# A state-space block's x projection: token-major products, turned by DMA transposes on ScalarE's queue

## The chip, the cores and the metric

The kernel runs on one core of one Trainium2 chip. The metric is device time in microseconds for one execution; the time of a kernel is the median of several runs. Engines are named as the profile names them: PE is TensorE (PEld its weight loads), DVE is VectorE, ACT is ScalarE, POOL is GpSimd, SP is SyncE, whose queue issues the weight loads. ACT has a DMA queue of its own (ACTq in the trace).

## The reference, cut to what matters

Two layers over 256 tokens of width 2048. Layer 0 is a differential attention, layer 1 a state-space mixer (Mamba-2); each is followed by a SwiGLU network. The change lies in the state-space mixer:

```python
proj = h @ w_in                                  # 256 x 2048 times 2048 x 10304
z, xbc, dt = jnp.split(proj, [4096, 10240], axis=-1)
xbc = silu(causal_conv(xbc, conv_w, width=4) + conv_b)   # per feature, along the tokens
xs, bm, cm = jnp.split(xbc, [4096, 5120], axis=-1)
...
y = ssd_chunked_scan(xs, dt, a, bm, cm)          # chunks of 128 tokens, 8 groups of 8 heads of 64
y = y + d_skip * xs
y = rms_norm(y * silu(z), norm_g)                # per group of 512 features
return y @ w_out
```

So of each of the 8 groups of 512 features, x is projected, convolved along the tokens, passed through silu, and used by tokens in the scan.

## The kernel before, in words

**Weight units.** All large products are split into three passes of reduced precision: a weight block is loaded by SP into one of seven buffers `raw` (128 x 1024, 512 KB), ACT copies it to a high part `wh` (`split_unit`, L260), and DVE subtracts to get the low part `wl`. `wh` and `wl` have four buffers each (`W_BUFS`), so ACT's copy for unit j+4 waits until PE has finished unit j. The activations have such a pair, `h` and `l` (`ah`, `al` in the trace). One unit covers 256 rows of the weight and 512 columns; a group's projection of 512 columns over 2048 rows is eight units.

**Two forms of a unit.** `products` (used by `push_k4`) keeps the activations stationary and streams the weights: 12 matmuls of 512 columns, and the result lies with tokens on the partitions. `feature_products` (used by `push_features`) keeps the weights stationary: 24 matmuls of 256 columns, and the result lies with features on the partitions. `Norm.push(..., features)` chooses: the fifth argument True gives the second form. In the first form the second matmul of a unit already reads `wl`; in the second the first 16 of 24 read `wh` alone.

**Order.** Everything is issued by one Python program, and each engine carries out its instructions in the order in which they were issued. Units enter a queue (`fifo`); `push_unit` issues the load and ACT's copy of a unit, and pops older units so that at most four wait. After the products of each popped unit `tick` runs one step of each generator in `active` (`step_all`), and, at a fixed rate, one of the `jobs` for the modulation vectors (one more `raw` load, and later a 128 x 1024 multiply on DVE, `raw<-raw,crow`). The subtraction for `wl` is issued one unit late (`lagging`, `low_parts`): that of unit j+3 is issued behind the step that follows unit j. Below, a step is the work issued after one unit, and step k of a group is the one after its k-th z unit; step 0 follows the last x unit.

**A group of the state-space stage.** Group g has eight x units (256-column form), `take_x` starts the generator `x_steps(g)`; then eight z units (512-column form), and `take_z` starts `y_steps(g)`. `x_steps` before: in steps 0 to 3 one tile of 128 features each goes through `conv_tile` (one ACT instruction from PSUM, L1555, three DVE instructions), in step 4 silu (L1565, with a load of ACT's function table ahead of it), in step 5 four PE transposes into a bank `wk`, and, once `y_steps(g-1)` is past its copies (`("done", g-1)`), two DVE multiplies; then the same for the second block of 128 tokens. `y_steps(g)` runs from step 8 on and into the next group: silu of z, 16 relu instructions in four steps, two exponentials with two DVE multiplies (`abc`), products `intra` on PE (the first in the next group's step 0), sums, two sums of squares (`square_sum`, steps 3 and 5), and from step 6 on the turning of y: ACT copies each y block's 32-bit words into two planes of 16-bit halves (L1772, `yT<-xsd`), and two `dma_start_transpose` on ACT's queue turn them into `yT` of the group (L1782). The place for the halves of group g is the not yet used `yT` of group g+1 (`y_turned(g+1)`).

**The output projection.** After z of group 7 come units (g, ch) of `ssd_out`, two units each, for groups g and output quarters ch. `split(cp, g)` prepares the stationary operand of a group ahead of it: for cp = 0 `y_words` first (two ACT copies that put the halves together, L383, and two DVE multiplies), then two ACT copies and two subtractions (L363). `split(0, 0)` is issued after the fourth z unit of group 7, `split(0, 1)` right after `take_z` of group 7, the next ones every four units. `flush_steps` runs all open generators to their end.

Of the kernel before, what the change touches and what calls it, by code (L numbers as in the profile page):

```python
# [11 lines left out]
F32 = mybir.dt.float32  # L12
# [3 lines left out]
U16 = mybir.dt.uint16  # L16
AF = mybir.ActivationFunctionType
# [75 lines left out]
def block_kernel(ctx: ExitStack, tc: tile.TileContext, x, x_t, columns_in, ssd_columns, da_columns, c, ada_w,  # L93
# [14 lines left out]
    pe, act, dve, pool, sp = nc.tensor, nc.scalar, nc.vector, nc.gpsimd, nc.sync  # L108
# [26 lines left out]
    rawp = ctx.enter_context(tc.tile_pool(name="rawp", bufs=RAW_BUFS))  # L135
# [8 lines left out]
    def bank(tag):  # L144
        return psum.tile([128, 512], F32, tag=tag, name=tag, bufs={"mm": 4, "wk": 3, "po": 1}[tag])

    def tmp(name="tmp"):
        return t2.tile([128, 512], F32, tag="t2", name=name)
# [19 lines left out]
    def take(what, n=1):  # L168
        while free[what] < n:
            yield  # L170
        free[what] -= n

    def give(what, n=1):
        free[what] += n
# [50 lines left out]
    def flush_steps():  # L225
        while active or pending:
            step_all()
# [131 lines left out]
    def split_act(parts):  # L359

        h, l = act_tiles()
        for at, src in parts:
            act.copy(at(h), src)  # L363
            dve.tensor_tensor(at(l), src, at(h).bitcast(F32), op=ALU.subtract)
        return blocks((h, l))
# [569 lines left out]
    wi = da_in  # L935
# [333 lines left out]
    for n in range(n_early, 12):  # L1269
        if n == n_early + 1:  # L1270
            call(load_x)
        hg, i = keys[n]
        bk = Banks()
# [251 lines left out]
    norm = Norm(0, mods["S", "m1"], mods["T", "m1"])  # L1525
# [23 lines left out]
    def tap(j, ct):  # L1549
        t = H[f"cw{j // 2}"]  # L1550
        i = (j % 2) * 48 + ct
        return t[:, i:i + 1]

    def conv_tile(src, d, ct):
        act.activation(d, src, AF.Identity, bias=H["cb"][:, ct:ct + 1], scale=tap(3, ct))  # L1555
        for j in range(3):
            m = 3 - j
            dve.scalar_tensor_tensor(d[:, m:], src[:, :256 - m], tap(j, ct), d[:, m:], op0=ALU.mult, op1=ALU.add)

    def conv_features(banks, n, dst, cts):  # L1560

        for k in range(n):
            conv_tile(banks[k // 2][:, (k % 2) * 256:(k % 2) * 256 + 256], dst[:, k, :], cts + k)
            yield
        act.activation(dst, dst, AF.Silu)  # L1565
        yield
# [99 lines left out]
    def hb(ap):  # L1666
        return ap[:, :, None].to_broadcast([128, 8, 64])

    def h3(ap):
        return ap.rearrange("p (h d) -> p h d", d=64)  # L1670

    def x_steps(g, banks):
        gp, h0 = S["gp"], 8 * g
        xc = gp.tile([128, 4, 256], F32, tag="xc", name="xc")
        yield from conv_features(banks, 4, xc, 4 * g)
        for b in range(2):
            yield from take("wk")
            ps = bank("wk")
            for i in range(4):
                pe.transpose(ps[:, i * 128:(i + 1) * 128], xc[:, i, b * 128:(b + 1) * 128], ident)  # L1680
            yield
            if b == 0:
                while g and ("done", g - 1) not in S:
                    yield
                xdt = S["xdt", g] = gp.tile([128, 2, 512], F32, tag="xdt", name="xdt")
                xsd = S["xsd", g] = gp.tile([128, 2, 512], F32, tag="xsd", name="xsd")
            dve.tensor_tensor(h3(xdt[:, b, :]), h3(ps), hb(S["dt"][:, b, h0:h0 + 8]), op=ALU.mult)
            dve.tensor_tensor(h3(xsd[:, b, :]), h3(ps), hb(H["dsk"][:, h0:h0 + 8]), op=ALU.mult)
            give("wk")
# [95 lines left out]
    def y_turned(g):  # L1785
        if ("yT", g) not in S:
            S["yT", g] = S["y0" if g < 4 else "y1"].tile([128, 2, 4, 128], F32, name=f"yT{g}")
        return S["yT", g]

    def half_tiles(t):  # L1790
        return t.rearrange("p k t -> p (k t)").bitcast(U16).rearrange("p (j t) -> p j t", t=128)
# [9 lines left out]
    wi = ssd_in  # L1801
    for col, n in ((9856, 448), (8192, 512), (8704, 384), (9088, 384), (9472, 384)):
        bk = Banks()
# [22 lines left out]
    hl = {}  # L1826

    def split(cp, g):
        if g == 7 and cp == 0:
            flush_steps()  # L1830
        if cp == 0:
            y_words(g)
        hl[cp, g] = split_act([(lambda t, b=b: t[:, :, b * 128:(b + 1) * 128], S["yT", g][:, b]) for b in range(2)])

    call(lambda: ada.update(rate=len(jobs) / ADA_UNITS))
    for g in range(8):
        bk = Banks()
        norm.push(wi, 4096 + g * 512, 512, bk, True)

        def take_x(g=g, bk=bk):  # L1840
            if g:
                step_until(xg[g - 1])
            xg[g] = start(x_steps(g, bk()))
        call(take_x)
        bk = Banks()
        norm.push(wi, g * 512, 512, bk, after=(lambda: split(0, 0)) if g == 7 else None)

        def take_z(g=g, bk=bk):
            yg[g] = start(y_steps(g, bk()))
        call(take_z)  # L1850
# [4 lines left out]
    def free_work():  # L1855
# [2 lines left out]
        phx = ExitStack()  # L1858
        nxt["xp"] = phx.enter_context(tc.tile_pool(name="xp_s", bufs=1))
        nxt["leave"] = lambda: (phx.close(), ph.close())  # L1860
    order = [(g, ch) for g in range(8) for ch in (0, 1)] + [(g, ch) for g in range(6) for ch in (2, 3)]
    order += [(6, 2), (7, 2), (6, 3), (7, 3)]
    bks = [Banks(t) for t in (("mm", "mm"), ("mm", "mm"), ("wk", "wk"), ("wk", "po"))]
    seen = []
    for g, ch in order:
        cp = ch // 2
# [5 lines left out]
    for g, ch in order:  # L1872
        cp = ch // 2
# [76 lines left out]
```

## Time and profile before

| | |
|---|---|
| median of 3 runs | 2609.04 us (2608.25 to 2609.65) |
| profiled execution: its time, its span | 2610.32 us, 2608.6 us |
| PE busy | 2584.8 us (99% of the span) |
| PEld / DVE / ACT / POOL busy | 2151.3 / 1914.4 / 1431.7 / 144.2 us |
| granted PE clock | 0.999 |
| DMA | 700.80 MB, mean 269 GB/s |
| state-space stage, groups 1 to 6 | 50.3 us each, PE busy throughout |

The profiled execution's time is its span and 1.7 us around it, and lies 1.3 us above the median. A busy sum adds up what overlaps inside an engine only once; the duration of one matmul in the trace (about 390 ns for 512 columns) is longer than the distance between two of them, since matmuls overlap. The rate of PE is therefore read from the chain of waits, where a row gives the start, the length and the number of matmuls in it.

### The profile page before, as it was taken

What the parts mean: (1) busy time and instruction counts of PE and PEld (TensorE: products, weight loads), DVE (VectorE), ACT (ScalarE), POOL (GpSimd) and SP (SyncE); (2) the same over time, 40 slices, a digit from 0 to 9 for tenths busy, and PEclk for the clock granted to TensorE, in tenths of its full rate; (3) what the DMA queues carried; (4) which work ended last, traced back from release to release, by engine and by line L of the source; (5) the groups of instructions that cost most, each with busy time, mean ns of one, the idle gap of its engine ahead of it and who ended that gap; (6) DMA issues with size and microseconds to landing.
All of it is one profiled execution on the core that took longest, in us unless ns stands there. A gap on an engine that the chain in (4) does not pass through costs nothing.

```text
span 2608.6 us, 35343 instructions
## 1 busy us (share of the span) xinstructions
PE 2584.8 (99%) x12914; PEld 2151.3 (82%) x12914; DVE 1914.4 (73%) x2621; ACT 1431.7 (55%) x1944; POOL 144.2 (6%) x227
## 2 busy tenths in 40 slices
PE   8999999999999999999999999999999999999999
PEld 5677778888888888888998899888888888888887
DVE  6778988778888867667777777786687664446775
ACT  4346654555654554446555676685545565545443
POOL 0014421000000000000000000010000000000000
PEclk9999999999999999999999999999999999999999
DMA  9977888698999988883667797876597687667885
GB/s 384 406 293 265 285 290 318 257 318 321 344 367 345 366 269 300 291 290 119 197 228 231 239 250 224 234 220 222 188 347 289 206 219 213 202 210 251 288 292 169
DMA packets 258206, 700.80 MB, mean 269 GB/s; under 512 B 86624, under 2 KB 95072, under 8 KB 256752
## 3 DMA queue, kind: packets, MB, share of 16 engines
q1 hardware_dynamic: 236176, 679.82, 76.4%
q10 hardware_dynamic: 17760, 4.43, 1.7%
q0 software_dynamic: 4096, 14.29, 1.6%
q8 instruction: 101, 1.65, 0.2%
q14 instruction: 73, 0.60, 0.1%
HBM read 680.53 MB, written 2.20 MB: 262 GB/s over the span
## 4 chain that ended last, share of the span: by engine, by line
PE 95%; DVE 2%; ACT 1%; issue 1%; DMA 1%; POOL 0%; POOLq 0%; ACTq 0%; DVEq 0%
PE mm L122 77%; PE wk L122 14%; PE po L122 5%; DVE wl L122 1%; DMA raw<-in_da_w_in 0%; DVE raw L122 0%; ACT wh L260 0%; ACT hm L563 0%; DVE xsum L122 0%; DVE partoh L122 0%; DVE x L122 0%; DVE hm L122 0%; DVE res L122 0%; POOL qr L415 0%; DVE qss L122 0%
## 5 line engine op out<-in xcount | busy, mean ns | idle before, releaser
L260 ACT CAST wh<-raw 128x1024 fp32r<-128x1024 f32 (+2 forms) x894 | 924.7, 1040 | 979.9 <-PE mm L122 615.3
L122 DVE TENSOR_TENSOR wl<-raw,wh 128x1024 fp32r<-128x1024 f32 (+2 forms) x894 | 1071.4, 1207 | 465.0 <-ACT wh L260 463.1
L122 PE MATMUL mm<-wh,ah 128*128 128x512 f32 (+1 forms) x2560 | 1012.0, 395 | 4.5 <-DVE partoh L122 2.9
L122 PE MATMUL mm<-wl,ah 128*128 128x512 f32 (+1 forms) x2560 | 997.9, 390 | 1.2 <-DVE wl L122 1.2
L122 PE MATMUL mm<-wh,al 128*128 128x512 f32 (+1 forms) x2560 | 998.9, 390 | 0.1
L122 PEld LDWEIGHTS mm<-wh,ah 128*128 128x128 f32 x2560 | 481.6, 188 | 130.3 <-issue 22.9
L122 PEld LDWEIGHTS mm<-wh,al 128*128 128x128 f32 x2560 | 481.4, 188 | 102.3 <-DVE al L122 1.3
L122 PEld LDWEIGHTS mm<-wl,ah 128*128 128x128 f32 x2560 | 481.9, 188 | 100.5 <-DVE wl L122 3.2
L122 DVE SCALAR_TENSOR_TENSOR raw<-raw,crow 128x1024 f32<-128x1024 f32 x320 | 389.7, 1220 | 0.0
L122 PE MATMUL wk<-wl,ah 128*128 128x512 f32 x360 | 140.1, 389 | 0.0
L122 PE MATMUL wk<-wh,al 128*128 128x512 f32 x360 | 140.1, 389 | 0.0
L122 PE MATMUL wk<-wh,ah 128*128 128x512 f32 x360 | 140.1, 389 | 0.0
L122 PE MATMUL mm<-ah,wh 128*128 128x256 f32 x720 | 118.8, 285 | 0.0
L122 PE MATMUL mm<-ah,wl 128*128 128x256 f32 x720 | 117.7, 283 | 0.0
L122 PE MATMUL mm<-al,wh 128*128 128x256 f32 x720 | 117.6, 283 | 0.0
L122 PEld LDWEIGHTS mm<-ah,wh 128*128 128x128 f32 x720 | 100.2, 192 | 0.1
L122 PEld LDWEIGHTS mm<-ah,wl 128*128 128x128 f32 x720 | 100.2, 192 | 0.0
L122 PEld LDWEIGHTS mm<-al,wh 128*128 128x128 f32 x720 | 100.1, 192 | 0.0
L505 POOL DMA_DIRECT2D gate_row<-grows x32 | 16.1, 509 | 1376.6 <-DVE grows L122 1376.6
L122 PEld LDWEIGHTS wk<-wl,ah 128*128 128x128 f32 x360 | 67.6, 188 | 14.2 <-DVE wl L122 0.2
L122 PEld LDWEIGHTS wk<-wh,al 128*128 128x128 f32 x360 | 67.6, 188 | 14.0
L122 PEld LDWEIGHTS wk<-wh,ah 128*128 128x128 f32 x360 | 67.6, 188 | 14.0
(331 smaller groups left out, 1998.3 us busy)
## 6 DMA issues: line engine op xcount, KB each, us to landing
raw<-in_ffn_w_gate_up SPq DMA_DIRECT2D x352, 512.0 KB, 4.9
raw<-in_ada_w SPq DMA_DIRECT2D x320, 512.0 KB, 5.2
raw<-in_ffn_w_down SPq DMA_DIRECT2D x176, 512.0 KB, 4.8
raw<-in_ssd_w_in SPq DMA_DIRECT2D x136, 512.0 KB, 4.5
raw<-in_da_w_in SPq DMA_DIRECT2D x90, 512.0 KB, 5.5
araw<-in_ada_w SPq DMA_DIRECT2D x64, 512.0 KB, 8.5
raw<-in_ssd_w_out SPq DMA_DIRECT2D x64, 512.0 KB, 4.4
raw<-in_da_w_out SPq DMA_DIRECT2D x32, 512.0 KB, 5.2
```

Source lines behind the costliest of these rows:

```text
L122: return fn(dst, *a, **k)
L260: act.copy(wh[:, at, :n], raw[:, at, :n])
L505: pool.dma_start(gate_dram[hf][:, 32 * q:32 * q + 32], rows[o:o + 8, :])
```

## The change

x of the state-space mixer is projected with tokens on the partitions (512-column form). `x_steps` then copies the two PSUM banks into halves (in the place of `xc`, which the convolution fills later), turns each block with a DMA transpose on ACT's queue, the second issued two steps after the first, puts the halves together with four ACT copies into two buffers `xin` of the common ring `t2`, and runs the convolution on these in two steps of two tiles, then silu, three empty steps, and the transposes on PE as before. The place for the turned halves is `y_turned(g+1)`, and for group 7 a buffer of `raw`. In the output projection group 7's first two quarters come after (0, 2) and (0, 3), and `flush_steps` is called at `split(1, 0)`.

```diff
     def x_steps(g, banks):
         xc = gp.tile([128, 4, 256], F32, tag="xc", name="xc")
-        yield from conv_features(banks, 4, xc, 4 * g)
+        hs = [xc[:, 2 * b:2 * b + 2, :].rearrange("p k t -> p (k t)").bitcast(U16) for b in range(2)]
+        for b in range(2):
+            act.copy(hs[b].rearrange("p (e f) -> p e f", e=2), banks[b].bitcast(U16).rearrange("p (f e) -> p e f", e=2))
+        if g < 7:
+            xT = [half_tiles(y_turned(g + 1)[:, b]) for b in range(2)]
+        else:
+            spare = rawp.tile([128, 2, 512], F32, tag="raw", name="xT")
+            xT = [half_tiles(spare[:, b].rearrange("p (k t) -> p k t", k=4)) for b in range(2)]
+        for b in range(2):
+            act.dma_start_transpose(xT[b], hs[b])
+            for _ in range(2 + b):
+                yield
+        for p in range(2):
+            xin = tmp("xin").rearrange("p (k t) -> p k t", k=2)
+            for b in range(2):
+                act.copy(xin[:, :, b * 128:(b + 1) * 128].bitcast(U16).rearrange("p k (t e) -> p k t e", e=2),
+                         xT[b].rearrange("p (e k) t -> p k t e", e=2)[:, 2 * p:2 * p + 2])
+            for i in range(2):
+                conv_tile(xin[:, i, :], xc[:, 2 * p + i, :], 4 * g + 2 * p + i)
+            yield
+        act.activation(xc, xc, AF.Silu)
+        yield
+        yield
+        yield
         for b in range(2):
             yield from take("wk")
...
-        if g == 7 and cp == 0:
+        if g == 0 and cp == 1:
             flush_steps()
...
-        norm.push(wi, 4096 + g * 512, 512, bk, True)
+        norm.push(wi, 4096 + g * 512, 512, bk)
...
-    order = [(g, ch) for g in range(8) for ch in (0, 1)] + [(g, ch) for g in range(6) for ch in (2, 3)]
+    order = [(g, ch) for g in range(7) for ch in (0, 1)] + [(0, 2), (0, 3), (7, 0), (7, 1)]
+    order += [(g, ch) for g in range(1, 6) for ch in (2, 3)]
     order += [(6, 2), (7, 2), (6, 3), (7, 3)]
```

## The prediction

> **What bounds the kernel now.** I read the page's first block, then the chain of waits, then the stage by windows, then the groups, tiles and timeline of ScalarE, because the first three say that only TensorE's own time counts here.
>
> ```profile
> span 2608.6 us, 35343 instructions
> PE 2584.8 (99%) x12914; PEld 2151.3 (82%) x12914; DVE 1914.4 (73%) x2621; ACT 1431.7 (55%) x1944; POOL 144.2 (6%) x227
> ```
>
> The profiled execution took 2610.32 us, its span 2608.6; the median of the runs is 2609.04. I make the sum against the profiled execution and subtract its 1.3 us at the end. PE is busy 99%. Two stretches of the chain give the price of both forms of a unit, and the windows show that the stage stands on PE alone:
>
> ```profile
> 978.42 10.88 PE mm L122 x48
> ...
> 1449.36 23.04 PE mm L122 x192
> ```
> ```profile
> core 0: us, PE busy (x) PEld busy (x) DVE busy (x) ACT busy (x) POOL busy (x), PEclk, DMA share, GB/s
> ...
> 1432.06:1482.36 50.30, 50.30 (x332) 45.80 (x331) 38.82 (x51) 32.98 (x50) 3.36 (x5) 1.00 0.78 243
> 1482.36:1532.65 50.29, 50.29 (x331) 45.79 (x331) 37.81 (x54) 32.96 (x50) 5.01 (x10) 1.00 0.87 228
> ```
>
> 48 matmuls of 512 columns take 10.88 us: 227 ns each, 2.72 us a unit of 12. The 192 matmuls of an x group take 23.04 us: 120 ns each, 2.88 us a unit of 24. A group is 50.3 us with no PE idle time; ACT is busy 33 of them, DVE 38, DMA for 0.78 to 0.87.
>
> **The change part by part.** *Products.* 64 x units go from 2.88 to 2.72 us: 64 x 0.16 = **10.2 us less** on PE, all on the path. The weights, their loads and copies are the same in number. PE's transposes, 8 a group, stay. That is the whole gain; the rest asks what makes PE wait.
>
> *ScalarE's bill.* These rows are of one group, and of all y tiles:
>
> ```profile
> L260 ACT CAST wh<-raw 128x1024 fp32r<-128x1024 f32 x17 | 17.8, 1047 | 18.6 <-PE mm L122 7.6 <-issue 7.6 <-DMA raw<-in_ssd_w_in 2.6
> L1555 ACT ACTIVATE xc<-mm,cb,cw 128x256 f32<-128x256 f32 x4 | 2.2, 557 | 1.6 <-DVE xc L122 1.6
> L1772 ACT COPY yT<-xsd 128x1024 uint16<-128x1024 uint16 x2 | 2.1, 1040 | 0.0
> L1565 ACT ACT_TABLE_LOAD x1 | 1.3, 1283 | 0.0
> L422 ACT ACTIVATE junk<-xsd 128x512 f32<-128x512 f32 x2 | 1.3, 626 | 0.0
> L1565 ACT ACTIVATE xc<-xc 128x1024 f32<-128x1024 f32 x1 | 1.1, 1061 | 0.0
> L1708 ACT ACTIVATE abc<-abc,acum 128x128 f32<-128x128 f32 x16 | 5.1, 393 | 0.2 <-issue 0.2
> ```
> ```profile
> L363 ACT CAST ah<-yT x32: 603/616/633, 1692.8 to 1860.8; 128x512 fp32r<-128x512 f32 x32
> L383 ACT COPY yw<-yT x16: 1157/1167/1185, 1690.6 to 1774.3; 128x1024 uint16<-128x1024 uint16 x16
> ...
> DMA to landing us min/median/max: 3.2/7.3/14.4
> ```
> ```profile
> L122 DVE SCALAR_TENSOR_TENSOR raw<-raw,crow 128x1024 f32<-128x1024 f32 x4 | 4.9, 1218 | 0.0
> L122 DVE SCALAR_TENSOR_TENSOR xc<-mm,cw,xc 128x255 f32<-128x255 f32 x4 | 1.9, 483 | 0.1
> ```
>
> Successive ACT records overlap by some 0.1 us (three copies in a row further down: 2.92 us, 0.96 each), so I count 0.96 for a copy of 1.05 and 1.2 for four relus. Added per group: two copies into halves, 0.95 each, and four copies that put halves together, each half of an L383 row: 0.55, 2.2 in all. The first pair falls in steps 0 to 4, where ACT waits for PE anyway: free. But in steps 5 to 7 there now stand the 2.2 us, the four convolution instructions (0.5 each, 2.0 in all, until now in steps 0 to 3), and table load with silu (2.25, until now in step 4). So 6.5 us more lie in three steps of 2.72 us, which already hold a weight copy each, a sum of squares (0.7) and a copy of y's halves (0.95). ACT can't work ahead: the copy of unit j+4 waits for PE's unit j, and what follows waits behind it.
>
> *A steady group.* Count from the end of z unit 4, when ACT copies unit 8. ACT: copy 0.96, squares 0.7, two xin copies 1.1, two convolution instructions 1.0, copy of unit 9 0.96, y's halves 0.95, 1.1, 1.0: 7.8 us. Behind the last but one of these DVE does two convolutions of three instructions (1.43 each by distance): 7.3 + 2.9 = 10.2, then `wl` of unit 9 (1.13, issued behind step 6): 11.3. PE wants that `wl` with its second matmul of unit 9, the next group's first x unit: 4 x 2.72 + 0.23 = 11.1. So 0.3 us late, or 1.5 where one of the four modulation multiplies of a group (1.22) falls in these steps. Before, the x unit's first 16 matmuls read `wh` alone, 1.9 us of grace that the new form gives up. Six handovers, two of them with the multiply: 4 x 0.3 + 2 x 1.5 = **4.2 us**. Bounds: 0 (if ACT and DVE are 0.3 us quicker from SBUF than from PSUM and no multiply falls there; the x records read PSUM) and 9 (all at 1.5).
>
> *Silu to PE.* Silu ends near 7.8 + 0.96 + 1.3 + 1.0 = 11.1 us; the transposes stand behind unit 10, at 16.3: 5 us of cover. With one step between, as before, PE would have waited 0.2. At step 10 `done` of the group before is past, so `wk` isn't held for three steps; nothing waited there, so nothing is won.
>
> *Group 7 and the first output units.* Here ACT has no spare time even now:
>
> ```profile
> 1695.00:1706.00 11.00, 11.00 (x51) 8.93 (x50) 9.55 (x13) 9.87 (x12) 1.85 (x2) 1.00 0.69 236
> 1706.00:1717.00 11.00, 9.99 (x44) 7.90 (x44) 8.17 (x11) 10.24 (x23) 0.00 (x0) 1.00 0.90 261
> 1717.00:1728.00 11.00, 11.00 (x58) 9.40 (x57) 10.54 (x13) 10.73 (x12) 0.00 (x0) 1.00 0.57 175
> ```
> ```profile
> 1700.61 1.05 ACT L260 CAST wh<-raw 128x1024 fp32r<-128x1024 f32 x1
> 1701.56 1.08 ACT L1702 ACTIVATE sz<-mm 128x512 f32<-128x512 f32 x2
> ...
> 1708.10 1.04 ACT L260 CAST wh<-raw 128x1024 fp32r<-128x1024 f32 x1
> ...
> 1723.18 2.92 ACT L260 CAST wh<-raw 128x1024 fp32r<-128x1024 f32 x3
> ```
> ```profile
> 1710.41 0.50 PE L122 MATMUL mm<-wl,ah 128*128 128x512 f32 x1 [1.01 <-DVE wl L122]
> ```
> ```profile
> 1673.56 1.73 PE wk L122 x16
> ...
> 1682.67 0.86 PE po L122 x2
> ...
> 1691.74 0.44 PE wk L122 x4
> ```
>
> Between the copies at 1700.61 and 1708.10 ACT carries silu of z, `split(0, 1)` and relus; PE waits 1.01 us for the `wl` behind them. With the change, from z unit 4's end on: copy 0.96, `split(0, 0)` 3.4, squares 0.7, xin and convolution 2.1, copy 0.96, y's halves 0.95, 2.1: 11.2 us. The next copy, of unit 10, waits for its load: group 7's turned halves lie in a `raw` buffer, and of the seven buffers this one is next in turn just for unit 10 (units 5 to 9 and one modulation block come between). The load can start when the second pair of xin copies has read the buffer, at 10.2, takes 0.3 to issue and lands 4.4 later:
>
> ```profile
> DMA to landing us min/median/max: 3.2/4.4/8.5
> ```
>
> So at 14.9, after 3.7 us of ACT idle, copy 0.96, table and silu 2.3, copy, y's halves, copy 2.9: 21.1; silu of z and `split(0, 1)` 4.4: 25.5; on DVE a subtraction, a multiply and `wl` of unit 12 (1.9 + 1.13): 28.5. PE wants it at 7 x 2.72 + 2 x 0.45 (transposes) + 0.23 = 20.2. Late by 8.3 in all (in parts, from unit 8 on). The next four units need 3.8 of copies, 4.8 of relus and 3.4 of `split(0, 2)` on ACT, 12.0 against PE's 10.9: 1.2 more. Less the 1.0 of before: **8.5 us**. Bounds: 3 (no late load, which is 3.7, and copies a little quicker) and 11.
>
> *DMA transposes.* Sixteen more, 256 KB each. ACT issues the second 5.4 us after x's last product (`intra` 1.73, one unit, one copy), and the xin copies stand at 16.9 (two `intra`, 0.86, four units, then copy and squares on ACT): a landing up to 11.5 us is covered, against the median of 7.3 above. Not all are that quick: while y's pair of group 2 is under way, bytes nearly stop,
>
> ```profile
> 1501.00:1503.00 2.00, 2.00 (x19) 2.00 (x18) 1.75 (x3) 2.00 (x6) 0.00 (x0) 1.00 1.34 114
> 1511.00:1513.00 2.00, 2.00 (x19) 2.00 (x18) 1.20 (x1) 1.98 (x2) 0.00 (x0) 1.00 1.51 96
> ...
> 1515.00:1517.00 2.00, 2.00 (x19) 2.00 (x18) 2.00 (x3) 1.55 (x3) 0.00 (x0) 1.00 1.00 393
> ```
> ```profile
> DMA to landing us min/median/max: 12.5/12.9/13.4
> ```
> ```profile
> DMA to landing us min/median/max: 13.2/13.8/14.4
> ```
>
> The second row is of group 5; with a median of 7.3 over all 16 the other groups are covered. At 12.9 and 13.8 ACT would wait 1.4 and 2.3 us, and PE nearly as long, as ACT has no slack in those steps. I take half of the 3.7, **2 us**, as x's pair goes out at another place among the loads. Bounds: 0 and 8 x 2.3 = 18. The Trainium skill's page "DMA: Bandwidth & Descriptors", section "Latency and other measured facts", gives a DMA transpose 261 GB/s of effective bandwidth; an estimate by it is 1.0 us for 256 KB, and then this term would be 0 and the sum 2 us lower. The trace disagrees: 3.2 us is its shortest landing.
>
> *Queues and the rest.* SP's queue gets no instruction, but waits for group 7's `raw` buffer (counted). ACT's queue issues 32 instead of 16 transposes; the new ones stand in steps 0 and 2, where ACT next waits for PE, so I cost their issue at nothing; in steps 5 to 7 it would be this much each:
>
> ```profile
> 1705.61 1.25 ACTq L1782 DMA_TRANSPOSE yT<-yT  x1
> ```
>
> POOL's `abc` load of 1 MB falls on step 4, after the x pair in most groups; it is needed from step 9 on. The new order of (7, 0) and (7, 1) and of `flush_steps` I cost at nothing: y of group 7 is issued by then in both, and PE has other units; PE was busy without a gap there:
>
> ```profile
> 1734.00:1794.00 60.00, 60.00 (x266) 49.66 (x265) 46.38 (x58) 40.45 (x50) 6.44 (x10) 1.00 0.77 232
> ```
>
> *Sum:* 2610.3 - 10.2 + 4.2 + 8.5 + 2 = 2614.8 for a profiled execution, **2613.5** as a median: no difference that 0.2% (5 us, about what a measurement of this kernel can tell from no change) would show, if only just.
>
> **The rivals.** *ScalarE keeps pace (faster).* The handovers stay whole and the first output units cost 3 us: 2609.0 - 10.2 + 3 = 2602. For it: ACT has 17 us idle a group, the change adds 4.1. Against: the idle time lies in steps 0 to 4 and 14 to 16. It decides if the load into the borrowed `raw` buffer isn't late and the 11.3 us shrink below 11.1.
>
> *Only the end costs.* Handovers whole, the end at 8.5 and the turning in time: 2607.3; with a few late landings 2609. Within 0.2%.
>
> *Landings late in every group (slower).* x's pair and y's pair go out nine units apart, and each is followed by a stretch at 400 GB/s that makes up for it; with two of them the loads run behind. At 13 us in all groups PE loses 1.5 us in each: 2613.5 - 2 + 12 = 2623.5. Against: DMA is at 0.78 to 0.87, and half of all land within 7.3 us.
>
> *The change doesn't do what it says:* x units in the new form stay at 2.88 us. Against: the 512-column units of the first row run at 2.72; the time would be 2613.5 + 10.2 = 2623.7.
>
> **How the numbers follow.** Forecast (2609 to 2620 by its own bounds) 0.43, about half of it above 2614.3; keeps pace 0.18; only the end 0.20; late in every group 0.17; no gain in the products 0.02. Faster by over 0.2%: 0.18. Within: 0.20 + 0.20 = 0.40. Slower: 0.23 + 0.17 + 0.02 = 0.42. Reaching to 2602 below and 2624 above leaves out about 2 in 10.
>
> **What the profile after would show.** x groups as 96 matmuls in 21.8 us; right after them, at the first matmuls of each next x group, PE waiting for DVE `wl`, 0.3 to 1.5 us; from the last z unit of group 7 to the fourth output unit PE idle 8 to 11 us, and one ACT copy waiting some 4 us for its load; landing of x's transposes, and ACT's xin copies waiting where it is over 11 us. The prediction is wrong if PE shows no idle time there (then 2602), if xin waits in every group, or if PE waits for the transposes of `xc`.

## The result, and the profile after

The changed kernel takes **2636.2 us** (median; 2628.7 to 2655.9) against 2609.3 of before in the same session: ratio 1.0115, interval 1.01 to 1.0129. It is slower by 1.1%, above the upper end of the forecast range (2624), and single executions differ by 27 us, where those of before stay within 4. The profiled one is among the short ones: 2630.05 us, span 2628.3, against 2610.32 and 2608.6. All of the 19.7 us lie in the state-space stage with its output projection: it lasts from 1249.75 to 1907.07 us (657.3) and lasted from 1250.23 to 1887.43 (637.2). The ratios of the experiments below, and e14's range, leave out an execution of e14 of 8697.8 us, which nothing here explains, and the two longest of e18.

Of the page's first block and its DMA queues, and of PE's waits in the stage (line, releaser: us in total, times, longest):

```profile
span 2628.3 us, 33899 instructions
PE 2583.0 (98%) x12146; PEld 2114.0 (80%) x12146; DVE 1914.2 (73%) x2621; ACT 1462.2 (56%) x1992; POOL 147.0 (6%) x227
...
q10 hardware_dynamic: 34656, 8.63, 2.8%
```
```profile
PE mm L122 <- DVE wl L122: 22.4, 9, 7.2
```

PE's busy time fell by only 1.8 us, although its work shrank (below), and it now waits 22.4 us for `wl`, where it waited 1.0. Queue q10 carries the transposes: twice the packets and bytes of before (17760, 4.43 MB).

The timeline of PE has the three kinds of gaps: group 0, a handover between two groups, and the end of the stage:

```profile
1350.97 0.79 PE L122 MATMUL mm<-wl,ah 128*128 128x512 f32 x1 [7.21 <-DVE wl L122]
...
1457.71 0.50 PE L122 MATMUL mm<-wl,ah 128*128 128x512 f32 x1 [1.72 <-DVE wl L122]
...
1507.84 0.50 PE L122 MATMUL mm<-wl,ah 128*128 128x512 f32 x1 [0.76 <-DVE wl L122]
...
1712.37 0.79 PE L122 MATMUL mm<-wl,ah 128*128 128x512 f32 x1 [6.53 <-DVE wl L122]
```

And the chain of waits names a transpose for the first and the last of these (its last row here is of the matmuls behind a further gap, of 2.24 us, at the end of the stage):

```profile
1328.80 16.66 DMA yT<-xc
...
1350.97 11.06 PE mm L122 x35
...
1415.79 13.65 PE mm L122 x60
...
1686.89 19.98 DMA xT<-xc
...
1728.16 15.28 PE mm L122 x59
```

In group 0 x's second transpose was under way for 16.7 us and in group 7 for 20.0; ScalarE stood at the `xin` copies that read it (timeline of ACT, group 0, and the other queue at the same time):

```profile
1338.24 0.68 ACT L1690 COPY xin<-yT 128x512 uint16<-128x512 uint16 x1 [1.78 <-DMA yT<-xc]
1345.48 0.67 ACT L1690 COPY xin<-yT 128x512 uint16<-128x512 uint16 x1 [6.56 <-DMA yT<-xc]
```
```profile
1324.60 0.59 POOL L1716 DMA_DIRECT2D abc<-acd  x1 [70.47 <-PE mm L122]
```

The last row is POOL's decay load `abc`, 1 MB, issued 2.0 us ahead of group 0's pair: it had waited for PE to release its buffer, which happens at the end of the x units. The windows around the gap, of a usual group and of the end show a third thing, the clock (PE's busy time is the first figure behind the length; the last three figures are the granted clock, the DMA share and GB/s):

```profile
1346.00:1348.00 2.00, 0.00 (x0) 0.00 (x0) 1.10 (x3) 1.97 (x4) 0.00 (x0) 0.70 0.68 272
1348.00:1350.00 2.00, 0.00 (x0) 0.00 (x0) 1.93 (x5) 1.97 (x5) 0.00 (x0) 0.50 0.06 23
1350.00:1352.00 2.00, 1.03 (x3) 0.84 (x4) 1.93 (x4) 1.43 (x3) 0.00 (x0) 0.50 0.06 12
1352.00:1354.00 2.00, 2.00 (x6) 1.61 (x5) 1.93 (x5) 0.13 (x1) 0.00 (x0) 0.50 0.71 250
1426.00:1476.00 50.00, 48.28 (x231) 39.79 (x230) 36.62 (x50) 36.08 (x55) 3.33 (x5) 1.00 0.81 239
1684.00:1753.40 69.40, 60.63 (x277) 49.30 (x276) 53.18 (x74) 51.88 (x74) 4.46 (x5) 0.93 0.79 204
```

PE idled 7.2 us and then ran at a clock of 0.50. The 35 matmuls of the row at 1350.97 took 11.06 us, and at 227 ns each they would take 7.95: 3.1 us lost behind the gap. In the window of a usual group (1426 to 1476), whose one gap is 1.72 us, the clock stays at 1.00. The Trainium skill, "TensorE: Matmul & The Clock Gate", section "Why this matters for your kernels", has the rule that a gap of PE of more than some 3 us puts the clock back to half. The trace agrees for the gaps of 7.21 and 6.53 us and for those of 1.72, but behind the gap of 2.24 us at 1728.16 the clock stood at 0.50 for 3.4 us too, so here less than 3 us was enough. My prediction had no term for the clock.

The account of the profiled execution: -9.6 us of PE's work (64 units at 2.73 instead of 2.88), +6.5 handovers (four of 0.76, two of 1.72), +7.2 group 0, +7.8 the end (8.8 us of idle in the last window, less the 1.0 of before). That is 11.9 of the 19.7. The other 7.8 us are inside PE's busy time, which fell by 1.8 us where the products alone took 9.6 off. Most of them are the lower clock: 3.1 behind group 0's gap, 1.5 behind the 6.53 us at the end (seven matmuls there start 0.40 to 0.59 us apart instead of 0.23), and 1.6 behind the 2.24 us (the 59 matmuls of the row at 1728.16 took 15.28 us, those of before 13.71). The rows don't tell where the last 1.6 us went.

### The profile page after: what moved, and what is told of

It reads as the page before. It is cut to its first block, busy times and chain, and to the rows that moved or that the text cites. A ratio compares the mean times of both kernels' runs of the same rounds, so it can differ in the third digit from the quotient of the medians.

```text
span 2628.3 us, 33899 instructions
## 1 busy us (share of the span) xinstructions
PE 2583.0 (98%) x12146; PEld 2114.0 (80%) x12146; DVE 1914.2 (73%) x2621; ACT 1462.2 (56%) x1992; POOL 147.0 (6%) x227
## 4 chain that ended last, share of the span: by engine, by line
PE 87%; DVE 4%; DMA 3%; ACT 3%; issue 1%; POOL 1%; ACTq 0%; DVEq 0%; POOLq 0%; SPq 0%
PE mm L122 69%; PE wk L122 13%; PE po L122 4%; DVE wl L122 1%; ACT wh L260 1%; DMA raw<-in_da_w_in 1%; DVE xc L122 1%; DMA xT<-xc 1%; DMA yT<-xc 1%; DMA raw<-in_ssd_w_in 1%; DVE raw L122 1%; ACT xin L1690 1%; ACT xc L1555 0%; DMA araw<-in_ada_w 0%; POOL rq L415 0%
## 5 line engine op out<-in xcount | busy, mean ns | idle before, releaser
L122 PE MATMUL mm<-wl,ah 128*128 128x512 f32 x2816 | 1100.8, 391 | 22.6 <-DVE wl L122 22.4
L122 PE MATMUL mm<-wh,ah 128*128 128x512 f32 x2816 | 1114.4, 396 | 4.4 <-DVE partoh L122 2.9
L122 PE MATMUL mm<-wh,al 128*128 128x512 f32 x2816 | 1101.0, 391 | 0.1
L122 PEld LDWEIGHTS mm<-wh,ah 128*128 128x128 f32 x2816 | 530.6, 188 | 140.4 <-issue 22.9
L122 PEld LDWEIGHTS mm<-wl,ah 128*128 128x128 f32 x2816 | 531.1, 189 | 135.9 <-DVE wl L122 27.4
L122 PEld LDWEIGHTS mm<-wh,al 128*128 128x128 f32 x2816 | 530.7, 188 | 112.7 <-DVE al L122 1.4
L383 ACT COPY aT<-turned 128x1024 uint16<-128x1024 uint16 x44 | 51.5, 1169 | 0.0
L122 PE MATMUL po<-wh,ah 128*128 128x512 f32 x120 | 46.9, 391 | 0.0
L122 PE MATMUL po<-wh,al 128*128 128x512 f32 x120 | 46.7, 389 | 0.0
L122 PE MATMUL po<-wl,ah 128*128 128x512 f32 x120 | 46.7, 389 | 0.0
```

The costliest lines, as they stand in the source:

```text
L122: return fn(dst, *a, **k)
L383: act.copy(dst.bitcast(U16).rearrange("p k (t e) -> p k t e", e=2), t.rearrange("p (e k) t -> p k t e", e=2))
```

## The experiments

Ratios are to the kernel before, run on the same chip beside each. A pair means x's two transposes of a group, a landing the time from a transpose's issue to its end. The first three columns are medians and the range in us.

| kernel | median | range | ratio [95%] |
|---|---|---|---|
| after | 2636.2 | 2628.7 to 2655.9 | 1.0115 [1.01, 1.0129] |
| e4_after_again (the same program) | 2637.6 | 2628.8 to 2646.5 | 1.011 [1.0089, 1.0132] |
| e1_no_wait | 2630.9 | 2616.9 to 2651.5 | 1.0089 [1.0053, 1.0124] |
| e2_pe_turn | 2609.4 | 2606.5 to 2610.1 | 1.0001 [0.9992, 1.0009] |
| e3_before_turns | 2618.5 | 2612.7 to 2621.3 | 1.0034 [1.0022, 1.0046] |
| e5_decay0_late | 2616.8 | 2608.9 to 2622.2 | 1.003 [1.002, 1.0039] |
| e6_abc_later | 2631.6 | 2621.2 to 2635.9 | 1.0077 [1.0061, 1.0093] |
| e7_wl_last | 2623.3 | 2616.8 to 2635.2 | 1.0062 [1.0038, 1.0085] |
| e8_spaced | 2607.4 | 2599.7 to 2612.4 | 0.999 [0.998, 0.9999] |
| e9_spaced_tied | 2600.5 | 2600.1 to 2605.0 | 0.9971 [0.996, 0.9982] |
| e10_before_turns_tied | 2608.9 | 2607.8 to 2609.5 | 1.0 [0.9991, 1.0008] |
| e11_after_tied | 2633.5 | 2622.3 to 2653.6 | 1.0102 [1.0068, 1.0136] |
| e12_g0_old | 2599.6 | 2598.6 to 2600.8 | 0.9964 [0.9952, 0.9976] |
| e13_close_pair | 2599.7 | 2599.2 to 2601.1 | 0.9964 [0.995, 0.9977] |
| e14_g7_turned | 2606.0 | 2603.3 to 2609.4 | 0.9988 [0.9979, 0.9997] |
| e15_wl_second | 2602.0 | 2600.8 to 2604.2 | 0.9972 [0.9961, 0.9984] |
| e16_abc_early | 2599.1 | 2598.3 to 2607.2 | 0.9968 [0.9958, 0.9979] |
| e17_bunch | 2608.6 | 2601.6 to 2622.0 | 1.0 [0.9987, 1.0013] |
| e18_later_groups | 2621.9 | 2600.9 to 2643.9 | 1.0035 [1.001, 1.006] |

**Is it the wait for the landing, the form of the products, or the transposes themselves?** In e1 the transposes are issued as in the change but turn other data, and `xin` is read from the halves as they lie, so x stays unturned in it:

```diff
-            act.dma_start_transpose(xT[b], hs[b])
+            act.dma_start_transpose(xT[b], xt[b][:, 0:512].bitcast(U16))
...
-                         xT[b].rearrange("p (e k) t -> p k t e", e=2)[:, 2 * p:2 * p + 2])
+                         hs[p].rearrange("p (e b k t) -> p b k t e", b=2, e=2, k=2)[:, b])
```

> The 16 transposes of x still run, into the same places, but from the residual tile, and ACT's xin copies read the halves before turning instead (x is left unturned), so nobody waits for a landing. Theory A (late landings hold ACT at xin, PE runs dry, and its granted clock then drops): what is left is the bunch of ACT work, 2609 - 9 + 6 + 8 = 2614 us, runs within 3 us of each other, PE never idle for over 4 us before group 7's end, granted clock 1.00 throughout the stage. Theory B (the added and moved ACT work alone): 2628 or more, as in the changed kernel. Theory C (the transposes' traffic makes weight loads late, whoever waits): 2622 or more, with ACT's weight copies waiting for raw.

e2 keeps the products by tokens and turns x on PE, as the kernel does elsewhere; no DMA transpose of x is left:

```diff
     def x_steps(g, banks):
...
-        for b in range(2):
-            act.dma_start_transpose(xT[b], hs[b])
...
+        yield from conv_tokens(banks, 4, xc, 4 * g)
```

> x's products by tokens, as in the changed kernel, but turned back by 8 PE transposes a group (the kernel's conv_tokens), two ACT copies ahead of them; no DMA transposes of x. Theories A and C: the products' gain of 9 us stays, the 64 transposes cost 64 x 0.11 = 7, no late landing: 2606 to 2609, runs within 3 us. Theory B as far as it is the token form itself that hurts (wl read by the second matmul of a unit): 1 us more in each group, 2614.

e3 is the kernel before, with two transposes a group in steps 0 and 2 (groups 0 to 6) whose results nobody reads, and e4 the change once more:

```diff
+        def turns():
+            for b in range(2):
+                act.dma_start_transpose(half_tiles(y_turned(g + 1)[:, b]), xt[b][:, 0:512].bitcast(U16))
+                yield
+                yield
+        if g < 7:
+            start(turns())
```

> The kernel before, with two DMA transposes a group added on ACT's queue in steps 0 and 2 for groups 0 to 6 (from the residual tile into the next group's yT), which nobody reads; the result is unchanged. Theory A: 2609 to 2611, PE idle no longer than before, although some pairs land after 12 us and more. Theory C: 2615 or more, ACT's weight copies waiting for raw in several groups.

> The changed kernel as it is, for a second profile. Theory A: 2628 to 2656 us; PE is idle over 4 us only in groups in which the later transpose of x landed after more than 11.5 us from its issue, and these need not be groups 0 and 7 again. Theory B: the same groups, 0 and 7, whatever the landings.

Without ScalarE waiting for them the transposes still cost most of it: 2630.9 us, with an interval that overlaps that of the change. In e1's waits of ACT the weights have taken their place:

```profile
ACT wh L260 <- DMA raw<-in_ssd_w_in: 28.9, 8, 13.0
```

So the transposes don't only land late, they make the loads beside them late (one more long wait of ACT in e1, 7.8 us, is for `gate_row`, small transfers on POOL's queue). e2 says that the products by tokens hurt nothing (2609.4): their gain is eaten by 64 more PE transposes (busy for 19.3 us instead of 9.6) and a wait of 2.6. And e3 shows the traffic alone, with neither the new products nor any work on ScalarE: 9 us slower, all of it in one place. ACT's and PE's waits, and group 0's pair:

```profile
ACT wh L260 <- DMA raw<-in_ssd_w_in: 18.9, 4, 11.6
```
```profile
PE mm L122 <- ACT wh L260: 8.5, 1, 8.5
```
```profile
DMA to landing us min/median/max: 21.7/24.8/27.9
```

The pairs of its groups 1 to 6 landed in 3.1 to 8.9 us, those of group 0 in 21.7 and 27.9, with the first decay load under way. The weights that PE's gap waited for were issued at 1333.87 and took some 24 us to land. (The transposes that nobody reads also hold up SP's queue: the profile puts 7.1 us of its waits in e3 and 14.7 in e1 down to their landings. In e3 that wait came after this load had been issued, so the load was slow on its way, not sent late.) e4 says that the change's stalls are not fixed in place: its pairs of groups 0, 2 and 6 landed at 20.9/24.3, 8.3/22.0 and, the second, at 17.4, with PE gaps of 15.2, 9.0 and 3.7; group 7's landed at 4.5 and 5.0, without the gap of 6.5.

**Taking things away one after the other.** e5 is e3 with the first decay load issued five steps later in the program; e6 the change with this and with the later decay loads behind POOL's reciprocal roots:

```diff
+        for _ in range(5):
+            yield
         load_decay(0)
...
-        if g < 7:
-            load_decay(g + 1)
         r = [rstd_of(ss[0], 1, 512, "yr")]
...
+        if g < 7:
+            load_decay(g + 1)
         square_sum(y[1], ss[1])
```

> The kernel before with two unread transposes a group (median 2618), and the first abc load (1 MB on POOL's queue, issued within 4 us of group 0's pair until now) five steps later. Theory D (a transpose is slow where it is in flight together with abc's load and the other transpose): group 0's pair lands within 10 us instead of 22 to 28, PE no longer waits 8 us there, 2609 to 2611 us. Theory C (any transpose beside the weight loads is slow at random): 2615 to 2621 as without the move.

> The changed kernel (median 2636) with the first abc load five steps later and the others one step later (step 5). Theory D: landings of x's pairs mostly under 11 us, PE idle over 4 us in at most one group besides the end, 2614 to 2622 us, of which 6 to 7 are the waits of 0.8 to 1.7 at the next group's first unit and 8 the end. Theory C: 2628 to 2650 as before.

e5 tells nothing on its question, because its edit moved nothing: POOL's queue is empty, so its load starts when the buffer comes free, in whichever step it is issued, and it still went out 0.4 us from group 0's first transpose (landings 18.8 and 23.3). The time stayed too. In e6 the later loads did move, from 2 to 8 us behind the pair, and group 0 (17.6, 23.2; a PE gap of 13.2) stayed as it was. Its 5 us against the change are hardly clear of the intervals (they overlap e4's).

e7 is e6 with the products that read `wl` last in each block of six; e8 is e7 with group 7 in the form of before, the transposes three steps apart, `xin` from step 7 on, one convolution tile a step, and two empty steps behind silu instead of three:

```diff
-            pe.matmul(ps[:, :n], h[:, k, :], wl[:, a, :n], start=False, stop=False)
-            pe.matmul(ps[:, :n], l[:, k, :], wh[:, a, :n], start=False, stop=last and a == tiles[-1])
+            pe.matmul(ps[:, :n], l[:, k, :], wh[:, a, :n], start=False, stop=False)
+        for a in tiles:
+            k = 2 * half + a
+            pe.matmul(ps[:, :n], h[:, k, :], wl[:, a, :n], start=False, stop=last and a == tiles[-1])
...
+        if g == 7:
+            yield from conv_features(banks, 4, xc, 4 * g)
...
-            for _ in range(2 + b):
+                for _ in range(3 + b):
...
                     conv_tile(xin[:, i, :], xc[:, 2 * p + i, :], 4 * g + 2 * p + i)
+                    if i == 0:
+                        yield
```

> The run before (abc later) with the two matmuls that read wl moved to the end of each block's six in every 512-column unit, so that wl is wanted 0.7 us later. Theory of the ACT bunch (wl late by 0.76, or 1.72 with a modulation multiply, at the first x unit): these waits become 0 and 1.0, 4 us less than with abc later alone. If the waits came from the landings they would stay: no difference.

> As the run before, and: group 7 in the old form (no borrowed raw buffer, no added ACT work ahead of the output projection), the second transpose three steps behind the first, xin read from step 7 on, one tile of the convolution a step, two empty steps behind silu. Theory D with the ACT bunch: the pair no longer overlaps, landings of up to 15 us are covered, no handover waits and the end as in the kernel before: 2609.3 - 7 x 1.15 = 2601 to 2604 us. Theory C: 2610 or more, weight copies waiting for raw.

e7's handover waits fell to two of 0.58; group 0 kept a gap of 7.6. (Its time fell by 8 us where 4 were expected, with intervals that overlap.) In e8 only group 0 stalls. ACT's and PE's waits, and its pair:

```profile
ACT wh L260 <- DMA raw<-in_ssd_w_in: 14.0, 1, 14.0
```
```profile
PE mm L122 <- ACT wh L260: 4.9, 1, 4.9
PE mm L122 <- DVE wl L122: 2.4, 1, 2.4
```
```profile
DMA to landing us min/median/max: 18.3/20.6/23.0
```

**Is it the decay load in group 0?** As a later issue doesn't move the load, e9, e10 and e11 tie it to the pair: a small POOL instruction reads the second turned half, and the load stands behind it on POOL's queue. Added to e8, e3 and the change:

```diff
-        load_decay(0)
...
+            if g == 0:
+                while "gq" not in S:
+                    yield
+                pool.tensor_copy(small(1, "yss").bitcast(U16), xT[1][:, 0, 0:2])
+                load_decay(0)
```

> Group 0's decay load (1 MB on POOL's queue) is tied behind the landing of x's pair by one small POOL instruction that reads the second turned half; all else as in e8_spaced (2607.4 us). Theory D (a pair of transposes and the decay load in flight together slow each other and the weight loads; group 0 is the one place left where they coincide): group 0's two landings fall from 18.3 and 23.0 us to under 11.5, its PE gaps of 4.88 + 2.41 us go, time 2598 to 2602 us. Rival R (group 0's pair is slow for another reason, such as being first in the stage or the weight loads around it): the landings stay at 17 us or more, the gaps stay, 2605 to 2609 us.

> e3_before_turns (the kernel before plus two transposes a group that nobody uses; 2618.5 us) with the first decay load tied behind the landing of group 0's pair in the same way. Theory D: group 0's landings fall from 21.7 and 27.9 us to under 11.5, the late weight load and the PE gap of 8.52 us go, 2609 to 2612 us: fourteen more transposes cost next to nothing where no decay load runs beside them. Rival R: gap and landings stay, 2616 to 2620 us.

> The kernel after (2636 to 2638 us) with that tie alone. Theory D: group 0's stall (7.2 us in one profile, 15.2 in another, and up to 3 us of lower clock behind it) goes, the chance stalls of later groups with transposes 1.4 to 2.6 us apart and the end's 6 to 9 us stay: 2620 to 2629 us. Rival R: 2634 to 2640 us.

e12 leaves the load where it was in e8 and takes the pair away, with group 0 by features:

```diff
-        if g == 7:
+        if g in (0, 7):
             yield from conv_features(banks, 4, xc, 4 * g)
...
-        norm.push(wi, 4096 + g * 512, 512, bk, g == 7)
+        norm.push(wi, 4096 + g * 512, 512, bk, g in (0, 7))
```

> e8_spaced with group 0 also in the form of before (by features, nothing turned), so that the first decay load meets no transpose. Theory D: no PE gap in group 0; one group's saving of 1.2 us is given up; 2599 to 2603 us, and groups 1 to 6 land as in e8_spaced (3 to 12 us). Rival R (the first pair of the stage is slow, wherever it is): group 1's pair takes over with 17 us or more and a stall, 2606 to 2610 us.

Group 0's pair in e9 and in e10, and e10's only wait of ACT for weights:

```profile
DMA to landing us min/median/max: 10.6/12.6/14.5
```
```profile
DMA to landing us min/median/max: 5.4/6.8/8.2
```
```profile
ACT wh L260 <- DMA raw<-in_ssd_w_in: 0.7, 1, 0.7
```

e10 loses all of e3's 9 us: its fourteen extra transposes cost nothing once no decay load runs beside the first two. e9 and e12 come out alike from the two sides, 7 and 8 us below e8, and beat the kernel before by 0.3 to 0.4%; the intervals of e10 and e12 are clear of those of e3 and e8, e9's just touches. (e9's second landing, 14.5, was over the 11.5 expected; ACT waited 1.9 us for it and PE 0.3.) So in group 0 the cause is shown: pair and decay load together. e11 misses its range, though: 2633.5, an interval that overlaps that of the change, so there the tie alone gains nothing that shows. In its profile group 0 is mended (landings 7.1 and 8.5) and another group is not:

```profile
ACT xin L1694 <- DMA yT<-xc: 12.9, 1, 12.9
```

This is group 5, landings 13.5 and 26.0, a PE gap of 12.3. The change's loss is mostly in other groups, at a place that differs from one execution to the next.

**What makes the later groups late?** e13, e14 and e15 take one mending each out of e9: the transposes two steps apart again (2.57 us in most groups as ACT's queue issues them, instead of 7.1), group 7 turned by DMA as in the change, `wl` second again.

```diff
-                for _ in range(3 + b):
+                for _ in range(2 + b):
```
```diff
-        if g == 7:
-            yield from conv_features(banks, 4, xc, 4 * g)
...
-        norm.push(wi, 4096 + g * 512, 512, bk, g == 7)
+        norm.push(wi, 4096 + g * 512, 512, bk)
```
```diff
+            pe.matmul(ps[:, :n], h[:, k, :], wl[:, a, :n], start=False, stop=False)
...
-        for a in tiles:
-            k = 2 * half + a
-            pe.matmul(ps[:, :n], h[:, k, :], wl[:, a, :n], start=False, stop=last and a == tiles[-1])
```

> e9_spaced_tied (2600.5 us) with the two transposes of a pair two steps apart again, as in the change, instead of three; the two steps go behind silu, so that all that follows stays where it was. Theory D (two transposes and the decay load in flight together): the real distance falls from 7.1 us to between 2.6 and 4.4, single groups stall in some executions, 2603 to 2612 us with a spread over 5 us. Rival S (the distance is nothing once the decay load of group 0 is out of the way; what e9 gained came from its other parts): 2599 to 2602 us, spread as in e9.

> e9_spaced_tied with group 7 turned by DMA as in the change (its products by tokens, its two transposes and its steps at the change's distances). Prediction's step for the end, as measured in the changed kernel (8.8 us of idle where before had 1.0): 1.2 us gained by the products, 6 to 9 lost: 2605 to 2609 us. Rival S (the end costs only where the transposes of group 7 are late through the queue of group 6 before it): 2598 to 2602 us.

> e9_spaced_tied with the products in the change's order (the low half of the weights read second, not last, in a block). If the handover waits for the low half depend on this order alone: 6 handovers at 0.76 or 1.72 us, 6.5 in all, 2605 to 2608 us. If they came from ScalarE's bunch of four convolution tiles, which is spread in this kernel: 0 to 2 us, 2600 to 2603 us.

The distance is nothing (rival S for e13), which is against what theory D said of the later groups. Group 7 costs 4 to 6 us (e9's ratio 0.9971, e14's 0.9988, with intervals that just overlap), its pair landing in 5.8 and 11.0 us; PE's waits in it, three of them (5.1 us) at the end:

```profile
PE mm L122 <- DVE wl L122: 6.6, 5, 2.2
```

And `wl` second costs nothing that shows (ratio 0.9972 against 0.9971; one wait of 1.0 us): where ScalarE's tiles are spread, the handovers have no wait to save. The last three go from e13 back towards e11: e16 with the later decay loads early again, e17 with two convolution tiles a step again, e18 with both and with the change's three steps behind silu (it differs from e11 by group 7 and the place of `wl` alone):

```diff
+        if g < 7:
+            load_decay(g + 1)
         r = [rstd_of(ss[0], 1, 512, "yr")]
```
```diff
                     conv_tile(xin[:, i, :], xc[:, 2 * p + i, :], 4 * g + 2 * p + i)
-                    if i == 0:
-                        yield
```

> e13_close_pair (2599.7 us; the pair 2.57 us apart, the next group's decay load 7 to 10 us behind its second transpose) with that load back in front of POOL's small reciprocal roots, as in the change, which puts it about 2 us behind. Theory D (both transposes of a pair and the decay load in flight together): pairs land at 10 to 26 us in single groups, stalls, 2603 to 2612 us and a spread over 5 us. Rival B (ScalarE's bunches make the stalls): 2599 to 2602 us.

> e13_close_pair with two convolution tiles in each of two steps, as in the change, instead of one in each of four (the two steps stand behind silu). Rival B (the four copies and four tiles that ScalarE works through in two steps delay the rounding of the next weights, so that a late load shows at once): 2603 to 2612 us and a spread over 5 us. Theory D: 2599 to 2602 us.

> e11_after_tied (2633.5 us) with only group 7 in the form of before and the low half of the weights last in each block, so that what is left of the change's loss in it belongs to groups 1 to 6: pair, decay load, bunches and the three steps behind silu as in the change. If the parts add up (6.4 us for group 7 by e14, 2.3 for the low half by e15): 2623 to 2627 us, with a spread over 8 us. If group 7 and the handovers themselves brought on the stalls of the other groups: 2600 to 2606 us.

e16 stays at 2599.1: the decay load 2.4 us behind a pair that is 2.57 us apart does no harm where the tiles are spread (one execution of 2607 apart), and there theory D is left with group 0 alone. e17 loses 9 us against e13 and its executions spread over 20: the two bunches of two copies and two tiles are one cause of the later stalls (rival B). e18 loses 20 against e13, 11 more than e17 (by a median of 2619.4 without its two longest executions), with intervals that just overlap; which of its two other edits adds these, or whether they only do so beside the bunches, was not tried. The parts add up about as foreseen: e11 less 6.4 and 2.3 (the medians of e14 and e15 against that of e13) is 2624.8, and e18 took 2619.4, or 2621.9 with all executions; with 43 us between its shortest and its longest this proves little. The version to keep is e16 or e13: the change with group 0's decay load tied behind its pair, group 7 as before, `wl` last, one tile a step and four steps behind silu, 9 to 10 us below the kernel before and some 37 below the change.

*How* the bunches make a transpose late is not settled. It is not the path that rival B names, weights rounded late: ACT waited 10.5 us for the landing itself. In group 4 of e17 ACT's instructions are those of e13 up to the `xin` copy that waits, and yet its pair landed in 11.1 and 23.7 us, e13's in 7.0 and 7.4. The windows of both, e17 first:

```profile
1521.00:1524.00 3.00, 3.00 (x19) 2.61 (x19) 2.58 (x4) 0.00 (x0) 1.37 (x3) 1.00 1.26 84
1527.00:1530.00 3.00, 3.00 (x15) 2.47 (x14) 2.75 (x4) 1.06 (x1) 1.08 (x2) 1.00 1.19 148
1533.00:1536.00 3.00, 3.00 (x15) 2.49 (x14) 0.00 (x0) 0.00 (x0) 0.00 (x0) 1.00 1.75 49
```
```profile
1521.00:1524.00 3.00, 3.00 (x17) 2.53 (x17) 1.82 (x2) 0.08 (x1) 0.00 (x0) 1.00 1.18 159
1527.00:1530.00 3.00, 3.00 (x15) 2.49 (x14) 2.75 (x4) 1.06 (x1) 1.22 (x3) 1.00 0.60 191
1533.00:1536.00 3.00, 3.00 (x15) 2.47 (x14) 2.16 (x4) 2.97 (x5) 0.00 (x0) 1.00 0.99 343
```
```profile
ACT xin L1699 <- DMA yT<-xc: 10.5, 1, 10.5
```
```profile
PE mm L122 <- DVE wl L122: 10.0, 3, 8.8
```

At 1533 to 1536 us e17's DMA engines count as more than full (1.75; the view counts a packet's whole time in the window in which it starts) and move 49 GB/s; e13's move 343. The y pair ahead of it had been slow too (9.7 and 19.1 us; 8.7 and 9.0 in e13), but that alone doesn't bring the state on: in e16 this y pair took 9.0 and 15.5 us, and the x pair behind it 6.7 and 7.1. Another candidate is in all these traces: four `gate_row` transfers of 1 KB that POOL's queue sends out with the pair of group 4. In e17 they went out 1.6 us later behind the pair's first transpose than in e13, and landed in 21 us instead of 5.5 to 6.7. Which event begins the state the rows don't show, and no run moved these transfers.

## Why the prediction was wrong

**Products: right.** 2.73 us a unit of 12 was measured (13.65 us for 60 matmuls), 0.15 saved where 0.16 was forecast: 9.6 for 10.2. The kernels without stalls keep it: e13 and e16 use the new form in seven groups, 8.4 us by these units, and are 9.4 and 9.6 us below before, whose one wait of 1.0 us they don't have.

**Steady handovers: right in kind, short in size.** Late `wl` at the next group's first x unit, small and large as forecast, but 0.76 and 1.72 for 0.3 and 1.5: 6.5 for 4.2. (The prediction's own sum, 11.33 less 11.11, gives 0.2, not 0.3.) A part of it is the `xin` copies, which I put at 0.55, half of an L383 row:

```profile
L1690 ACT COPY xin<-yT x28: 664/677/684, 1338.2 to 1653.7; 128x512 uint16<-128x512 uint16 x28
```

**Silu to PE: right.** PE never waited for the transposes of `xc`.

**Group 7 and the first output units: right in size by luck, half by another cause.** 8.8 us of idle where 8.3 + 1.2 = 9.5 was worked out, 7.8 net for 8.5. The wait for the load into the borrowed `raw` buffer, 3.7 us of it, did not come: the load went out at 1711.75, as the last `xin` copy had read the buffer, and landed 4.4 us later, but ACT copied this unit only at 1726.97. ACT's one wait for weights of `ssd_out` (first row) came later, at 1791.0, where PE doesn't wait; at the end of the stage it waited for x instead (second row):

```profile
ACT wh L260 <- DMA raw<-in_ssd_w_out: 3.4, 1, 3.4
ACT xin L1690 <- DMA xT<-xc: 3.6, 1, 3.6
```

x's second half landed at 1706.9 (20.0 us), and the first weights of `ssd_out`, issued beside it, at 1707.0 (19.6 us): late landings again, in the gap of 6.53 us. In e4, e6, e7, e11 and e14, where group 7's pair landed in 4.5 to 11.0 us, PE's waits at the end are 5.0 to 5.6 us together, 4.0 to 4.6 net, near the 4.8 that the prediction's 8.5 leaves without its 3.7.

**DMA transposes: the step that failed.** Its working was: covered up to a landing of 11.5 us, 1.4 and 2.3 us beyond, half of the sum taken, 2 us. Three things in it were wrong. First, it took the landings of y's transposes as those of x's; the median held (7.1 for 7.3), the tail did not: 16.7 and 20.0 here, 22 to 26 in e4 and e11.

```profile
DMA to landing us min/median/max: 3.1/7.1/20.0
```

Second, it noted the decay load "on step 4, after the x pair in most groups" and priced it at nothing; in group 0 the load goes out with the pair, and e3 and e10 put 9 us on that alone (in the change itself e11 shows no such gain: its stalls came up in other groups). Third, it counted only ACT's wait for the landing. In e1 and e3 ACT has no such wait, and they are still 22 and 9 us above before, with weights that land late; and behind a gap of 7 us PE ran at half its clock for some us, which no term had. The bound of 18 stood in the text, but taken for eight landings of 13 us, not for single ones of 20; with it and the other terms as measured the sum would have reached 2632, still below the median. The rival "landings late in every group" named the right mechanism with the wrong shape: not each group a little, but one to four of them a lot, and others in each execution.

One row had shown it: y's pairs of before at 12.5 to 14.4 us with the bytes at 96 to 114 GB/s. I read these as a delay of two transfers. As I read them now, they are the state of e17's windows, harmless in the kernel before because PE waited for nothing there (no run tests this reading). The Trainium skill, "Advanced Engine Details and Errata", section "X-Bar Transpose (TRN2)", has transposes as fast as regular DMAs and expects 350 to 400 GB/s. The rows disagree where transposes run beside the weight stream: 49 GB/s in e17's last window.

**The order of the output units and of the flush: right at nothing.** From the end of the row of 12 matmuls behind group 7's last `intra` products to the end of the stage before takes 154.2 us (1733.2 to 1887.4) and after 154.5 (1752.6 to 1907.1). Behind the stage both take 721.2 us.

## What to carry to other kernels

A transfer that lands in time in the median still has to be priced by its tail, and by what it does to the streams beside it: issue it where nobody needs it, in a kernel that doesn't need it, as in e3, and time that first. Look for what else is released by the same event (here the end of the x units frees the decay buffer and the pair's source), and if the two collide, tie one behind the other by a real dependence, since an idle queue ignores a later place in the program. With that tie, group 7 left as it was, `wl` read last and ScalarE's new work spread to one tile a step instead of two, the change was worth 0.3 to 0.4%.

## What the runs showed of the hardware

- DMA engines that count as busy for 1.75 of a window moved 49 GB/s (e17); in the same place of e13, at 0.99, 343. The busy share is no measure of what moves while transposes are under way.
- 256 KB turned inside the core's memory took 3.1 to 27.9 us from issue to landing in these runs, next to the same stream of weights.
- After 6.5 to 7.2 us without a matmul the granted clock was 0.50 and back at 1.00 some 3 to 6 us after work resumed; gaps of up to 1.72 us left it at 1.00. In between it went either way: a gap of 2.4 to 2.5 us near 202 us, which every profile here has, was followed by 3.4 us at 0.50 in 14 of the 20 profiles (that of before among them) and left the clock at 1.00 in 6 (e16 among them).
- One program without any change of data differed by 43 us between executions (e18), where the kernel before differed by 3.
